# Channel mixing of a hybrid decoder layer: plain products, or seven block products with sums on VectorE

## The chip, the cores and the metric

The kernel runs on one core of a Trainium2 chip. Its time is the device time of one execution in microseconds (us). It is given as the median of several runs, and the trace is of one execution more, recorded by the profiler.

## What is computed

One decoder layer for 1024 tokens of width 1024, all in float32. Two token mixers (an RWKV-7 recurrence and a forgetting attention) are merged, projected and added to the residual stream; then comes the channel mixing, the only part that changes:

```python
h2 = _modulate(x, norm2_g[l], sh2, sc2)                      # (1024 tokens, 1024)
ff_out = jnp.square(jax.nn.relu(h2 @ w_ff1[l])) @ w_ff2[l]   # 1024 -> 4096 -> 1024
x = x + gt2[:, None, :] * ff_out
...
return _rmsnorm(x, final_g)
```

## The kernel before

TensorE multiplies float32 as three products of rounded parts. Each operand is split into a rounded high part and the remainder: ScalarE makes the high part by a copy (`ACT.copy`), VectorE subtracts it from the whole. The helper `mm` (L41) is called three times for each product, high by high, low by high, high by low, and every matmul in the trace has its line. A matmul here is 128x128 weights by 512 columns into one bank of PSUM.

Ahead of the channel mixing stands the output projection (`p_out`, L1095 to L1104), for pairs of 128-token tiles. For each tile VectorE multiplies by the gate (L1108) and adds the residual (L1109), giving x1; SP writes x1 to DRAM (`x1_d`, L1110); then come a sum of squares, a reciprocal root and a scaling of the tile `xr` (L1113). After every fourth tile TensorE transposes (L1120), ScalarE applies scale and shift (L1122) and copies the high part (`hhi`, L1123), VectorE makes the low part (`hlo`, L1124). The channel mixing then holds all of h2, transposed, as `hhi` and `hlo`.

The 4096 hidden channels are 32 blocks of 128. `up(n)` (L1140 to L1152) makes one of them for all 1024 tokens: SP loads 512 KB of `w_ff1` (`wr_f`, L173), it is split (L176, L177), 48 matmuls fill `p_f`, ScalarE takes relu and square (`rl`, `fh`), VectorE makes the low part `fl`. `w2(n)` (L1154 to L1165) loads the 512 KB of `w_ff2` that belong to it (`w2r`), POOL multiplies them by the gate `gt2` (L1157), and they are split (`w2h`, `w2l`). `down(g)` (L1181 to L1198) takes two blocks: for each of 8 token tiles and 2 halves of the output 12 matmuls into one bank `o`, which VectorE adds to `acc` (L1193). `acc` begins as x1, read back from DRAM (L1137). The last two calls are taken together, and `finish(t)` (L1171) normalises a tile and sends it out.

The order is written out by hand at the end of the part: up and down alternate, two blocks each.

```python
for g in range(NG + 1):
    ...
        ups.append(up(2 * g + 2))
    if g < NG - 1:
        down(g, ups[gs], w2s[gs])
    if g < NG:
        ups.append(up(2 * g + 3))
        w2s += [w2(2 * g + 2), w2(2 * g + 3)]
```

A scheduler then fixes the order of each engine's queue, and adds the waits: an engine carries out its queue in order, and a queue of DMA issues (SP's, or POOL's) stands still while its first entry waits.

Of the kernel before, what the change touches and what calls it, by code (L numbers as in the profile page):

```python
# [8 lines left out]
F32 = mybir.dt.float32  # L9
F32R = mybir.dt.float32r  # L10
# [6 lines left out]
P = 128  # L17
# [18 lines left out]
def build(ctx, tc, A, out):  # L36
# [13 lines left out]
    actp = ctx.enter_context(pool(name="actp", bufs=1))  # L50
# [986 lines left out]
    wos = []  # L1037

    def wo_load(dp, k):
        raw = dp.tile([P, D], F32, tag="dr", name=f"wr_out{k}", bufs=4)  # L1040
        POOL.dma_start(raw, wout[k])
        return raw
# [9 lines left out]
    with pool(name="yp", bufs=1) as yp, pool(name="gp", bufs=1) as gp:  # L1052
# [19 lines left out]
        for _ in fill:  # L1072
            pass
        dpa = dax.enter_context(pool(name="dpa", bufs=1, side="right"))
        raws = [wo_load(dpa, k) for k in range(4)]
# [7 lines left out]
    with pool(name="dp", bufs=1) as dp:  # L1083
        for k in range(4, KT):
            wo_split(dp, k, wo_load(dpa, k))
        ssq = dp.tile([P, 8], F32, name="ssq2")
        rs2 = dp.tile([P, 8], F32, name="rs2")
        rtmp = dp.tile([P, 16], F32, name="rtmp2")
        x1s = []
        for t in range(8):  # L1090
            ts_ = slice(t * P, (t + 1) * P)
            if t % 2 == 0:
                os_ = [big(f"p_out{t + i}") for i in range(2)]
                for ks in (range(4), range(4, KT)):
                    for i in range(2):  # L1095
                        tt = slice((t + i) * P, (t + i + 1) * P)
                        for hf in range(2):
                            o, sl = os_[i], slice(hf * 512, hf * 512 + 512)
                            for k in ks:
                                wh, wl = wos[k]  # L1100
                                mm(o[:, sl], hhi[:, k, tt], wh[:, sl], k == 0, False)
                                mm(o[:, sl], hlo[:, k, tt], wh[:, sl], False, False)
                                mm(o[:, sl], hhi[:, k, tt], wl[:, sl], False, k == KT - 1)
            o = os_[t % 2]  # L1104
            xt = dp.tile([P, D], F32, tag="x1", name=f"xr{t}", bufs=5)
            SP.dma_start(xt, x_t[t])
            t1 = dpa.tile([P, D], F32, tag="dr", name=f"t1{t}", bufs=4)
            DVE.tensor_tensor(t1, o, gt1, ALU.mult)  # L1108
            DVE.tensor_tensor(xt, xt, t1, ALU.add)  # L1109
            SP.dma_start(x1_d[t], xt)  # L1110
            ACT.activation(t1, xt, AF.Square, accum_out=ssq[:, t : t + 1])
            rsqrt(rs2[:, t : t + 1], ssq[:, t : t + 1], 1.0 / D, eps1, rtmp[:, 2 * t : 2 * t + 2], 1)
            DVE.tensor_scalar(xt, xt, rs2[:, t : t + 1], None, ALU.mult)  # L1113
            x1s.append(xt)
            if t % 4 == 3:
                sl = slice((t - 3) * P, (t + 1) * P)
                for k in range(KT):
                    hp_ = bank(f"hp{t}_{k}")
                    for i in range(4):
                        PE.transpose(hp_[:, i * P : (i + 1) * P], x1s[t - 3 + i][:, k * P : (k + 1) * P], ident)  # L1120
                    hr = dpa.tile([P, 512], F32, tag="dr", name=f"hr2{t}_{k}", bufs=4)
                    ACT.activation(hr, hp_, AF.Identity, bias=sh2[:, k : k + 1], scale=sc2[:, k : k + 1])  # L1122
                    ACT.copy(hhi[:, k, sl], hr)  # L1123
                    DVE.tensor_tensor(hlo[:, k, sl], hr, hhi[:, k, sl].bitcast(F32), ALU.subtract)  # L1124
    dax.close()


    ff1 = A["w_ff1"].rearrange("o (k p) n -> p (o k) n", p=P)
    ff2 = A["w_ff2"].rearrange("o (k p) n -> (o k) p n", p=P)
    G = 2  # L1130
    with pool(name="fp", bufs=1) as fp:
        fg = gt1
        SP.dma_start(fg, A["final_g"].rearrange("(o n) -> o n", o=1).broadcast_to([P, D]))
        acc = []
        for t in range(8):
            a_ = fp.tile([P, D], F32, name=f"acc{t}")
            SP.dma_start(a_, x1_d[t])  # L1137
            acc.append(a_)

        def up(n):  # L1140
            o = proj(load_w(ff1[:, :, n * P : (n + 1) * P], 0, KT, f"f{n}"), f"p_f{n}")
            rl = fp.tile([P, S], F32, name=f"rl{n}", tag="rl", bufs=2)
            ACT.activation(rl, o, AF.Relu)  # L1143
            if n < NFF - 1:
                fh = fp.tile([P, S], F32R, name=f"fh{n}", tag="fh", bufs=3)
                fl = fp.tile([P, S], F32R, name=f"fl{n}", tag="fl", bufs=3)
            else:
                fh, fl = [wp.tile([P, S], F32R, name=f"f{x}{n}", tag="wraw", bufs=2) for x in "hl"]
            ACT.activation(fh, rl, AF.Square)
            DVE.tensor_tensor(rl, rl, rl, ALU.mult)  # L1150
            DVE.tensor_tensor(fl, rl, fh.bitcast(F32), ALU.subtract)
            return fh, fl  # L1152
# [28 lines left out]
        def down(g, fs, ws):  # L1181
            last, n = g == NG - 1, len(fs)
            for t in range(8):
# [13 lines left out]
                if last:  # L1197
                    finish(t)  # L1198
# [37 lines left out]
```

## Time and profile before

| | us |
|---|---|
| runs | 1756.55, 1750.68, 1753.89 |
| median | 1753.89 |
| the profiled execution, its own time | 1749.61 |
| its span in the trace | 1747.6 |
| output projection ends, channel mixing begins | 1036.25 |
| last matmul ends | 1739.81 |

PE is TensorE's matmuls, DVE VectorE, ACT ScalarE, POOL GpSimd, SP the engine that issues most DMAs. The span is the time from the first to the last instruction; the execution's own time has 2.0 us around it. The page of the profile gives busy time by engine, the span in 40 slices of 43.7 us, and the chain of work that ended last: followed back from the end, at each step to what released it. A group of equal instructions is told by line, engine, operation, output and inputs, with its count, its time and the mean of one.

### The profile page before, as it was taken

The page shows a single profiled execution, that of the slowest core. Times are in us where ns is not written, and L with a number is a line of the kernel's source. Part 1 is how long each engine was busy: PE and PEld are TensorE (multiplying, and loading weights), DVE is VectorE, ACT ScalarE, POOL GpSimd, SP SyncE. Part 2 cuts the span into 40 slices and gives each one's busy share as a digit, 9 for nine tenths or more (in the row PEclk, how much of TensorE's full clock was granted, in tenths as well). Part 3 has the DMA queues.
Part 4 walks back from the last instruction along what each step waited for, and adds up shares of the span by engine and source line. Part 5 has one row for each costly group of instructions (what it writes and reads, how often), then busy time and mean ns, then how long its engine had stood idle before and what let it go on. Part 6 is the DMA issues. An engine that isn't in the chain of part 4 may idle for free.

```text
span 1747.6 us, 21804 instructions
## 1 busy us (share of the span) xinstructions
PE 1671.4 (96%) x8677; PEld 1350.8 (77%) x8677; DVE 971.1 (56%) x1500; ACT 570.3 (33%) x869; POOL 368.3 (21%) x265
## 2 busy tenths in 40 slices
PE   3999999999999999999999999999999999999998
PEld 2767776777777778888877888888888888888886
DVE  6676664647656655766657446444444444444436
ACT  5453342435545523332333323111111111111122
POOL 4310000899990012221100002111111111111100
PEclk9999999999999999999999999999999999999999
DMA  8435335421223278877767134111111111111102
GB/s 249 126 112 154 109 99 161 121 61 61 67 70 103 73 232 240 249 235 232 248 204 247 75 125 137 49 48 49 48 49 49 49 49 49 48 49 48 37 12 96
DMA packets 205907, 197.50 MB, mean 113 GB/s; under 512 B 28113, under 2 KB 170730, under 8 KB 205678
## 3 DMA queue, kind: packets, MB, share of 16 engines
q1 hardware_dynamic: 204302, 189.55, 35.9%
q0 software_dynamic: 1296, 6.29, 1.0%
q8 instruction: 68, 1.11, 0.3%
q14 instruction: 33, 0.27, 0.0%
q10 hardware_dynamic: 208, 0.28, 0.0%
HBM read 148.80 MB, written 43.09 MB: 110 GB/s over the span
## 4 chain that ended last, share of the span: by engine, by line
PE 81%; DVE 5%; DMA 4%; ACT 2%; issue 1%; POOL 0%; SPq 0%; DVEq 0%; ACTq 0%
PE o L41 20%; PE p_f L41 20%; PE p_gb L41 5%; PE p_out L41 4%; PE p_ga L41 3%; PE my L41 3%; PE p_ob L41 2%; PE p_fq L41 2%; PE p_fv L41 2%; PE p_fk L41 2%; PE p_v L41 2%; PE yv L41 2%; PE p_r L41 2%; PE p_k L41 2%; PE tp L818 2%; PE s L41 1%
## 5 line engine op out<-in xcount | busy, mean ns | idle before, releaser
L1193 DVE TENSOR_TENSOR acc<-acc,o 128x512 f32<-128x512 f32 x240 | 162.1, 686 | 193.8 <-PE o L41 193.8
L1157 POOL TENSOR_TENSOR w2r<-w2r,gt 128x1024 f32<-128x1024 f32 x32 | 77.3, 2431 | 721.8 <-DMA w2r<-in_w_ff 721.7
L41 PE MATMUL p_f<-hlo,wh_f 128*128 128x512 f32 x512 | 200.0, 391 | 0.0
L41 PE MATMUL p_f<-hhi,wl_f 128*128 128x512 f32 x512 | 199.6, 390 | 0.0
L41 PE MATMUL p_f<-hhi,wh_f 128*128 128x512 f32 x512 | 199.5, 390 | 0.0
L41 PE MATMUL o<-w2h,fl 128*128 128x512 f32 x496 | 193.4, 390 | 0.0
L41 PE MATMUL o<-w2l,fh 128*128 128x512 f32 x496 | 193.2, 390 | 0.0
L41 PE MATMUL o<-w2h,fh 128*128 128x512 f32 x496 | 193.0, 389 | 0.0
L1143 ACT ACTIVATE rl<-p_f 128x1024 f32<-128x1024 f32 x32 | 32.9, 1028 | 268.4 <-PE p_f L41 268.4
L177 DVE TENSOR_TENSOR wl_f<-wr_f,wh_f 128x1024 fp32r<-128x1024 f32 x32 | 41.1, 1284 | 142.3 <-ACT wh_f L176 142.3
L1163 ACT CAST w2h<-w2r 128x1024 fp32r<-128x1024 f32 x31 | 31.1, 1050 | 251.4 <-PE o L41 251.4
L41 PEld LDWEIGHTS p_f<-hlo,wh_f 128*128 128x128 f32 x512 | 96.1, 188 | 20.4 <-DVE hlo L1124 0.5
L41 PEld LDWEIGHTS p_f<-hhi,wl_f 128*128 128x128 f32 x512 | 96.1, 188 | 20.2
L41 PEld LDWEIGHTS p_f<-hhi,wh_f 128*128 128x128 f32 x512 | 96.1, 188 | 20.0
L41 PEld LDWEIGHTS o<-w2h,fl 128*128 128x128 f32 x496 | 93.1, 188 | 20.0
L41 PEld LDWEIGHTS o<-w2h,fh 128*128 128x128 f32 x496 | 93.1, 188 | 19.8
L41 PEld LDWEIGHTS o<-w2l,fh 128*128 128x128 f32 x496 | 93.1, 188 | 19.5
L638 POOL TENSOR_TENSOR dg<-dg,inv 128x62 f32<-128x62 f32 (+30 forms) x62 | 100.2, 1616 | 4.8
L637 POOL TENSOR_TENSOR inv<-dg 128x62 f32<-128x62 f32 (+30 forms) x62 | 93.0, 1500 | 4.9
L822 DVE TENSOR_TENSOR pl<-tp,ph 128x512 fp32r<-128x512 f32 (+1 forms) x80 | 49.2, 632 | 24.8 <-ACT ph L821 24.6
L700 POOL TENSOR_TENSOR sw<-sbd,wcs 64x256 f32<-64x256 f32 x28 | 22.9, 818 | 168.0 <-DVE sbd L701 137.5
L880 ACT ACTIVATE pt<-pt,sm 128x128 f32<-128x128 f32 (+3 forms) x64 | 49.5, 775 | 24.5 <-DVE sm L878 23.5
(466 smaller groups left out, 3729.8 us busy)
## 6 DMA issues: line engine op xcount, KB each, us to landing
aw<-in_w_ada SPq DMA_DIRECT2D x32, 512.0 KB
wr_f<-in_w_ff SPq DMA_DIRECT2D x32, 512.0 KB
w2r<-in_w_ff SPq DMA_DIRECT2D x32, 512.0 KB
wa<-in_w_ada SPq DMA_DIRECT2D x16, 512.0 KB
sc_d<-scb SPq DMA_DIRECT2D x16, 512.0 KB
sct<-sc_d SPq DMA_DIRECT2D x16, 512.0 KB
x<-in_x SPq DMA_DIRECT2D x8, 512.0 KB
ar_d<-ar SPq DMA_DIRECT2D x4, 1024.0 KB
```

Source lines behind the costliest of these rows:

```text
L41: PE.matmul(o, l, r, start=start, stop=stop)
L177: DVE.tensor_tensor(lo, raw, hi.bitcast(F32), ALU.subtract)
L637: POOL.tensor_tensor(tv, dg[:, 0:s, s : s + 1].broadcast_to([P, s, m]), dg[:, s : s + 1, s + 1 :].broadcast_to([P, s, m]), ALU.mult)
L638: POOL.tensor_tensor(dg[:, 0:s, s + 1 :], dg[:, 0:s, s + 1 :], tv, ALU.add)
L700: POOL.tensor_tensor(sw[rs], cur[rs, :, rs], wcs[rs, :, c : c + 1].broadcast_to([64, 4, 64]), ALU.mult)
L818: PE.transpose(tp[:, x * P : (x + 1) * P], pr[b][:, t * P : (t + 1) * P], ident)
L822: DVE.tensor_tensor(pl[:, 0:w_], tp[:, 0:w_], ph[:, 0:w_].bitcast(F32), ALU.subtract)
L880: ACT.activation(pt[:, 0:n], pt[:, 0:n], AF.Exp, bias=low, scale=-1.0, accum_out=ls[:, b : b + 1])
L1143: ACT.activation(rl, o, AF.Relu)
L1157: POOL.tensor_tensor(raw, raw, gt2, ALU.mult)
L1163: ACT.copy(wh, raw)
L1193: DVE.tensor_tensor(acc[t][:, sl], acc[t][:, sl], o, ALU.add)
```

## The change

The product of two matrices, each cut into 2x2 blocks, is made of seven block products in place of eight, in Winograd's form: sums and differences of the blocks of either factor are multiplied, and the products are summed. This is done for the way up and for the way down.

Up: the factors are the weights of two neighbouring blocks of channels (a "pair", 16 of them: `A11` to `A22` for halves of the input width and the two blocks; S1 to S4 their sums) and the activations (`B11` to `B22` for halves of the width and of the tokens; T1 to T4 their sums). A product is 12 matmuls (`up_product`). The products S1 and S4 go into a bank `y`, S2, S3, A22 and the first one into a bank `x`, the second first one into a bank `z`; between the products ScalarE copies the partial result out of the bank into `ff0` to `ff3`, and VectorE adds the final state to it. In the first two pairs the two are taken through each product together, and T1 to T4 are made in between.

Down: the hidden values are the first factor. Per pair seven operands of 128x512 (`A11`, `A12`, `A22`, S3, S1, S2, S4) are written by POOL's queue to DRAM (`f_put`, 112 of 256 KB). The way down follows the whole way up: 4 groups of 4 pairs, 7 steps each; a step is 4 token tiles of 12 matmuls, with 1 MB of hidden values (`load_a`) and in some steps 1 MB of `w_ff2` (`load_b`) by SP. VectorE multiplies the blocks of `w_ff2` by `gt2` (`scale_b`, which POOL did), makes their sums T, the low parts (`fl`, `wl`), and adds each step's banks to `acc` (`evict`); the residual x1 is added in groups 1 and 2 (`residual`). Step 0 of the way down has its loads and splits within the last pair of the way up (`start_down`, `start_split`).

```diff
+    for t in range(8):
...
+                if t == 4:
+                    for j in range(2):
+                        if ks[0] == 0:
+                            first_ops(j)
+                        else:
+                            for name in ("S1", "S3", "S2", "S4"):
+                                rest_sum(j, name)
...
+    def up_product(o, w, b, start):
+        (wh, wl), (bh, bl) = w, HB[b]
+        for k in range(4):
+            mmx(o, wh[:, k], bh[:, k], start and k == 0, False)
+            mmx(o, wl[:, k], bh[:, k], False, False)
+            mmx(o, wh[:, k], bl[:, k], False, k == 3)
...
+    for k in range(4):
+        DVE.tensor_tensor(t1f[:, k], h2b[0][:, k], hi("B11", k), ALU.subtract)
+        DVE.tensor_tensor(t1f[:, k], t1f[:, k], lo("B11", k), ALU.subtract)
+        DVE.tensor_tensor(t2f[:, k], h2b[1][:, k], t1f[:, k], ALU.subtract)
+        t_split("T1", k, t1f)
...
+    def up_step(j, name):
+        x = X[j]
+        if name == "S1":
+            Y[j] = bank(f"y{j}", "y")
+            up_product(Y[j], rest.pop((j, "S1")), "T1", True)
+            ACT.copy(f_tile(j, 3), Y[j])
+        elif name == "S2":
+            up_product(x, rest.pop((j, "S2")), "T2", False)
+            ACT.copy(f_tile(j, 1), x)
+        elif name == "S4":
+            up_product(Y[j], rest.pop((j, "S4")), "B22", False)
+        elif name == "S3":
+            up_product(x, rest.pop((j, "S3")), "T3", False)
+            DVE.tensor_tensor(Fb[j, 3], x, Fb[j, 3], ALU.add)
+            f_square(j, 3)
+            f_put(j, "A22", Fb[j, 3])
+        else:
+            up_product(x, rest.pop((j, "A22")), "T4", False)
+            ACT.activation(f_tile(j, 2), x, AF.Relu)
+            f_square(j, 2, False)
+            f_put(j, "A12", Fb[j, 2])
...
+    for j in range(2, NPAIR):
+        last = j + 1 == NPAIR
+        if j + 2 < NPAIR:
+            raw_pair(j + 2)
+        if last:
+            start_down()
+        up_step(j, "S1")
...
+        up_step(j, "A22")
...
+    for name in ("S1", "S2", "S4"):
+        f_sum(NPAIR - 1, name)
...
+        STEPS = [
+            ("y", True, "A12", "B21", [(0, 0)]),
+            ("x", True, "A11", "B11", [(0, 0)]),
+            ("y", True, "S1", "T1", [(1, 1)]),
+            ("x", False, "S2", "T2", [(0, 1)]),
+            ("y", False, "S4", "B22", [(0, 1)]),
+            ("x", False, "S3", "T3", [(1, 1)]),
+            ("x", False, "A22", "T4", [(1, 0)]),
+        ]
...
+            if i == 1:
+                scale_b("B11")
+            elif i == 2:
+                scale_b("B12")
+                R["T"] = fp.tile([P, 4, 512], F32, name=f"T_{g}", tag="T", bufs=1)
+                DVE.tensor_tensor(R["T"], R["B12"], R["B11"], ALU.subtract)
...
+            src = R[("B21", "B11", "T", "T", "B22", "B12", "T")[i]]
+            h_, l_ = [to.tile([P, 4, 512], F32R, name=f"w{x}{g}_{i}", tag=f"w{x}", bufs=2) for x, to in (("h", fr), ("l", fp))]
+            split(h_, l_, src)
...
+        for s, (g, i) in enumerate(flat):
+            loads(s + 3)
+            prepare(s + 1)
+            if i == 5 and g + 1 < NG:
+                load_b(g + 1, "B21")
+            if g == NG - 1 and i == 0:
+                fg = dpp.tile([P, D], F32, name="fg", tag="gt1", bufs=1)
+                SP.dma_start(fg, A["final_g"].rearrange("(o n) -> o n", o=1).broadcast_to([P, D]))
+            tag, opens, _, _, to = STEPS[i]
+            fa, wb = ops.pop(s)
+            for t in range(4):
...
+                for half, d in to:
+                    evict(o, t + 4 * half, d, s > 0)
...
+            if g in (1, 2) and i >= 3:
+                residual(4 * (g - 1) + i - 3)
```

What the scheduler makes of it stands in the queues. ScalarE's queue in the middle of the way up, before: casts of the weights down, relu, cast of the weights up, square.

```order
L1163 CAST w2h29_12948<-w2r29_12945 128x1024
L1163 CAST w2h30_13079<-w2r30_13076 128x1024
L1143 ACTIVATE rl29_12931<-p_f29_12882 128x1024
L176 CAST wh_f31_13016<-wr_f31_13014 128x1024
L1149 ACTIVATE fh29_12933<-rl29_12931 128x1024
```

The same queue after, from the end of pair 4 into pair 5 (`ur7` is the raw block of pair 7, `uwhi7` its high part, `y5` the bank of S1 and S4, `x4` and `x5` the banks of the others):

```order
L1320 ACTIVATE ff2_4_9944<-x4_9800 128x512
L1093 CAST A22h_5_9948<-ur5_9665 128x512
L1240 ACTIVATE ff2_4_9944<-ff2_4_9944 128x512
L1239 ACTIVATE ff0_5_9923<-ff0_5_9923 128x512
L1240 ACTIVATE ff0_5_9923<-ff0_5_9923 128x512
L1093 CAST uwhi7_10139<-ur7_9969 128x512
L1307 COPY ff3_5_9985<-y5_9972 128x512
L1093 CAST S1h_6_10018<-S_6_10014 128x512
```

The cast of a raw block of weights (`uwhi7`) now stands ahead of a copy out of PSUM (`ff3_5`), after which TensorE goes on in that bank; before, a bank was read once, when it was complete.

SP's queue where the way up ends. Before, at the end of the part, loads for up and down in turn and the output:

```order
L173 DMA wr_f30_12952<-in_w_ff1 128x8x128
L1156 DMA w2r29_12945<-in_w_ff2 128x1024
L1156 DMA w2r30_13076<-in_w_ff2 128x1024
L173 DMA wr_f31_13014<-in_w_ff1 128x8x128
L1156 DMA w2r31_13083<-in_w_ff2 128x1024
L1179 DMA out_y<-acc0_9071 128x1024
```

After, at the beginning of the way down (`f_d` is the DRAM copy of the hidden operands, `dA1` that of step 1):

```order
L1497 DMA dA3_11639<-f_d_9050 128x4x512
L1555 DMA x1t0_12412<-x1_d_8379 128x1024
L1555 DMA x1t1_12481<-x1_d_8379 128x1024
L1503 DMA B22_0_11641<-in_w_ff2 128x4x512
L1605 DMA fg_13140<-in_final_g 128x1024
L1497 DMA dA1_11633<-f_d_9050 128x4x512
L1503 DMA B11_0_11634<-in_w_ff2 128x4x512
L1497 DMA dA2_11631<-f_d_9050 128x4x512
L1503 DMA B12_0_11632<-in_w_ff2 128x4x512
```

The load of `fg`, written for the last group, has moved ahead of the loads of steps 1 and 2; it takes the memory of the tile `ft15`, whose last write to DRAM it waits for.

VectorE's queue in the way down. Before, evictions one behind the other, with the splits of the next blocks between them:

```order
L1193 TENSOR_TENSOR acc7_9085<-acc7_9085,o8_7_0_11530 128x512
L1193 TENSOR_TENSOR acc7_9085<-acc7_9085,o8_7_1_11538 128x512
L1164 TENSOR_TENSOR w2l19_11619<-w2r19_11615,w2h19_11618 128x1024
L1164 TENSOR_TENSOR w2l20_11878<-w2r20_11874,w2h20_11877 128x1024
L177 TENSOR_TENSOR wl_f21_11815<-wr_f21_11812,wh_f21_11814 128x1024
```

After, around the steps 3 to 5 of group 1:

```order
L1094 TENSOR_TENSOR wl1_4_12357<-B22_1_12134,wh1_4_12356 128x2048
L1583 TENSOR_TENSOR fl11_12353<-dA11_12204,dh11_1_12350 128x1024
L1545 TENSOR_TENSOR acc0_11668<-x1_1_0_12220,acc0_11668 128x512
L1545 TENSOR_TENSOR acc1_11683<-x1_1_1_12234,acc1_11683 128x512
L1556 TENSOR_TENSOR acc0_11668<-acc0_11668,x1t0_12412 128x1024
L1511 TENSOR_TENSOR B21_2_12500<-B21_2_12500,gt2_5349 128x2048
L1545 TENSOR_TENSOR acc2_11698<-x1_1_2_12248,acc2_11698 128x512
L1511 TENSOR_TENSOR B22_2_12630<-B22_2_12630,gt2_5349 128x2048
```

Between the evictions now stand scalings, sums and splits of 128x2048, and the residual.

## Rows read from the trace of the kernel before

**Rows 1.** Page: span, busy time by engine, the span in 40 slices.
```profile
span 1747.6 us, 21804 instructions
...
PE 1671.4 (96%) x8677; PEld 1350.8 (77%) x8677; DVE 971.1 (56%) x1500; ACT 570.3 (33%) x869; POOL 368.3 (21%) x265
...
PE   3999999999999999999999999999999999999998
```

**Rows 2.** The chain of waits from 950 us on: start, us, what.
```profile
1036.25 0.02 issue
...
1043.19 0.76 DVE xr L1113
...
1048.94 24.74 PE p_f L41 x108
1073.68 21.80 PE o L41 x96
...
1739.81 0.02 issue
```

**Rows 3.** Windows: us, busy PE, PEld, DVE, ACT, POOL, granted clock, DMA share, GB/s.
```profile
950.00:955.00 5.00, 3.29 (x12) 1.70 (x10) 4.03 (x6) 3.91 (x5) 0.00 (x0) 0.96 0.86 306
955.00:960.00 5.00, 4.99 (x16) 3.96 (x16) 2.32 (x3) 0.50 (x1) 0.00 (x0) 0.70 0.62 238
...
1044.00:1060.00 16.00, 16.00 (x79) 12.84 (x80) 7.63 (x9) 12.53 (x19) 2.82 (x2) 1.00 0.74 290
...
1200.00:1300.00 100.00, 100.00 (x441) 82.61 (x441) 46.34 (x56) 18.62 (x19) 9.54 (x4) 1.00 0.16 48
```

**Rows 4.** Timeline of DVE, 1205 to 1212 us: start, us, instruction.
```profile
1205.97 0.69 DVE L1193 TENSOR_TENSOR acc<-acc,o 128x512 f32<-128x512 f32 x1 [6.66 <-PE o L41]
1206.57 1.23 DVE L177 TENSOR_TENSOR wl_f<-wr_f,wh_f 128x1024 fp32r<-128x1024 f32 x1
1207.71 1.22 DVE L1150 TENSOR_TENSOR rl<-rl 128x1024 f32<-128x1024 f32 x1
```

**Rows 5.** DVE's groups by shape: count, busy us, mean ns, idle before.
```profile
L1193 DVE TENSOR_TENSOR acc<-acc,o 128x512 f32<-128x512 f32 x240 | 162.1, 686 | 193.8 <-PE o L41 193.8
...
L1164 DVE TENSOR_TENSOR w2l<-w2r,w2h 128x1024 fp32r<-128x1024 f32 x31 | 36.5, 1218 | 0.0
...
L177 DVE TENSOR_TENSOR wl_fv<-wr_fv,wh_fv 128x1024 fp32r<-128x1024 f32 x4 | 9.7, 2418 | 0.3 <-ACT wh_fv L176 0.3
...
L588 DVE TENSOR_TENSOR bk<-bk,wcs 128x2048 f32<-128x2048 f32 x4 | 9.1, 2269 | 0.0
```

**Rows 6.** ACT's groups by shape, the same columns.
```profile
L1163 ACT CAST w2h<-w2r 128x1024 fp32r<-128x1024 f32 x31 | 31.1, 1050 | 251.4 <-PE o L41 251.4
...
L1122 ACT ACTIVATE hr<-hp,sh,sc 128x512 f32<-128x512 f32 x16 | 11.7, 789 | 6.6 <-PE hp L1120 6.6
...
L1123 ACT CAST hhi<-hr 128x512 fp32r<-128x512 f32 x16 | 9.2, 635 | 0.0
```

**Rows 7.** Timelines of SP and of POOL, 1226 to 1234 us: a load, its first use.
```profile
1228.23 1.48 SPq L1156 DMA_DIRECT2D w2r<-in_w_ff  x2
...
1231.52 4.86 POOL L1157 TENSOR_TENSOR w2r<-w2r,gt 128x1024 f32<-128x1024 f32 x2 [38.90 <-DMA w2r<-in_w_ff]
```

**Rows 8.** The same timelines, 1036 to 1075 us.
```profile
1039.75 5.13 SPq L1137 DMA_DIRECT2D acc<-x_d  x8
1052.43 0.81 SPq L1156 DMA_DIRECT2D w2r<-in_w_ff  x2
...
1057.18 5.75 POOL L1157 TENSOR_TENSOR w2r<-w2r,gt 128x1024 f32<-128x1024 f32 x2 [186.12 <-DMA w2r<-in_w_ff]
```

**Rows 9.** Instructions of line 1041, loads by POOL's queue: min, median, max ns; landing.
```profile
L1041 POOL DMA_DIRECT2D wr_out<-in_w_out x8: 540/540/608, 843.8 to 870.5; - x8
...
DMA to landing us min/median/max: 4.4/6.7/9.6
```

More of the change, by code (lines that the diff above doesn't have):

```diff
@@ L1082, in build @@
     x1_d = dram.tile([8, P, D], F32, name="x1_d")
[L1083 to L1124, printed above, removed]
@@ new lines, in build, with f_put, f_tile, f_square @@
+    AOPS = ("A11", "A12", "A22", "S3", "S1", "S2", "S4")
+    f_d = dram.tile([len(AOPS), NPAIR, P, 512], F32, name="f_d")
+    X, Z, Y, Fb, Fs = {}, {}, {}, {}, {}
+    def f_put(j, name, src):
+        POOL.dma_start(f_d[AOPS.index(name), j], src)
+    def f_tile(j, b):
+        Fb[j, b] = up_.tile([P, 512], F32, name=f"ff{b}_{j}", tag=f"ff{b}", bufs=1 if b == 2 else 2)
+        return Fb[j, b]
+    def f_square(j, b, relu=True):
+        f = Fb[j, b]
+        if relu:
+            ACT.activation(f, f, AF.Relu)
+        ACT.activation(f, f, AF.Square)
@@ new lines, in first_second, with first_first, first_out @@
+    def first_second(j):
+        wh, wl = first[j]
+        Z[j] = bank(f"z{j}", "z")
+        up_product(Z[j], (wh[:, 4:8], wl[:, 4:8]), "B21", True)
+    def first_first(j):
+        wh, wl = first[j]
+        X[j] = bank(f"x{j}", "x")
+        up_product(X[j], (wh[:, 0:4], wl[:, 0:4]), "B11", True)
+    def first_out(j, which):
+        if which == 0:
+            ACT.copy(f_tile(j, 0), Z[j])
+        else:
+            DVE.tensor_tensor(Fb[j, 0], X[j], Fb[j, 0], ALU.add)
+            f_square(j, 0)
+            f_put(j, "A11", Fb[j, 0])
@@ L1169, in build @@
         rtmp = fp.tile([P, 16], F32, name="rtmp3")
+        x1ts = {}
+        STEPS = [
[7 more added lines that the diff above has]
+        ]
+        flat = [(g, i) for g in range(NG) for i in range(7)]
@@ new lines, in build, with evict @@
+        seen = set()
+        def evict(o, t, d, scaled):
+            sl = slice(512 * d, 512 * d + 512)
+            if t >= len(acc):
+                acc.extend(fp.tile([P, D], F32, name=f"acc{t_}") for t_ in range(len(acc), t + 1))
+            if (t, d) in seen:
+                DVE.tensor_tensor(acc[t][:, sl], o, acc[t][:, sl], ALU.add)
+            else:
+                seen.add((t, d))
+                if scaled:
+                    ACT.copy(acc[t][:, sl], o)
+                else:
+                    DVE.tensor_tensor(acc[t][:, sl], o, gt2[:, sl], ALU.mult)
@@ L1200, in build @@
[L1200 to L1212 removed]
+        BL = {1: "B11", 2: "B12", 3: "B22"}
```

422 lines of the change are left out of this document (351 added, 71 removed).

## The prediction

> **What bounds the kernel now.** I began with the busy shares and the slices of the span [rows 1]. They say that TensorE (PE) is the engine to save on: it is busy 96% of the span, 9 tenths or more in every slice but the first and the last. Then I followed the chain of waits through the channel mixing, the only part that changes [rows 2]. From 1048.94 us to 1739.81 it is TensorE alone: `p_f`, two blocks up, 96 matmuls, `o`, two blocks down, 96, and so on without a wait between. One matmul of 128x512 takes 21.80/96 = 0.2271 us there. The part starts when the output projection ends, at 1036.25; 3072 matmuls are 697.7 us and 32 transposes some 3.5, of 703.6 us in all, so 2.4 us are lost, all around the last tile `xr7`, which is ready only at 1043.95. The stretches confirm it [rows 3]: between 1200 and 1300, PE 100 of 100 us at the full clock, VectorE (DVE) 46, ScalarE (ACT) 19, GpSimd (POOL) 10, DMA 16%. A saved matmul is thus worth its full 0.2271 us, as long as the other engines, now with room, keep up.
>
> **Matmuls removed.** Seven products replace eight: TensorE's queue has 6868 rows instead of 7252, 384 matmuls of 128x512 fewer. 384 x 0.2271 = **87.2 us** [rows 2]. A pair of channel blocks takes 84 matmuls, 19.1 us; a step down (48) 10.9 us. All else is what the other engines give back of that.
>
> **The opening, +4.5.** The way up needs sums of the activations, T1 to T4, that exist only after the last transpose. TensorE's products with the first half of the tokens, 48 matmuls (10.9 us), cover the wait for `xr7`. From the last transpose to the end of the last T4 split, DVE has 55 operations of 128x512. Back to back such operations start 0.60 us apart [rows 4], though each takes 0.69 [rows 5]: 33.0 to 38 us, plus 0.8 for the first ACT copy out of PSUM [rows 6]. Beside them TensorE has 141 matmuls, 32.0 us, of which about 8 come after the last split. So 33.8 or 38.8 less 30.2: 3.6 to 8.6 us lost, a little more where a copy waits its turn on ACT, against 2.4 lost before. I take 4.5 net; ends +1 and +11.
>
> **The way up, +2.** Per pair DVE has 18 operations of 128x512, 10.8 us at the pitch of [rows 4], and ACT 18 of 0.64 to 0.79 us [rows 6], 12 to 14: both fit in 19.1. What is tight is one load. The raw block of the pair after next may be fetched only when split A22l of this one is done: after the product A22, ACT's relu 0.79, a cast 0.64, DVE's subtraction 0.69 [rows 5, 6], some 2.1 us. On ACT the cast of that block, `uwhi`, stands ahead of the copy `ff3` out of bank y, which TensorE needs before product S4, 36 matmuls or 8.2 us after A22. So the first half, 512 KB, must land within 8.2 - 2.1 - 0.64 - 0.79 = 4.6 us. A load of that size by SP was used 3.3 us after its issue [rows 7], and 4.8 us after it where 4 MB of other loads went ahead [rows 8]. The first costs nothing, the second 0.15 us in each of 13 pairs, 2 us. I take 2; ends 0 and +13 (1 us a pair). The 112 writes of the results into DRAM go through POOL's queue, 0.54 us of issue each [rows 9], 3.8 us a pair on an engine that now does nothing else here.
>
> **From up to down, +15.** This is the new wait. Step 1 down loads operands that only the last pair completes. Count from E0, the end of step 0; the last product up ends 38 matmuls, 8.6 us, earlier. Relu, square and DVE's last difference end at -6.5 (0.79, 0.64, 0.69); its write takes at least 4.4 us, the shortest POOL transfer in the trace [rows 9], and ends at -2.1. On SP's queue the load of `fg` waits for exactly this write, as it takes that tile's memory; behind it stand `dA1`, `B11`, `dA2`, `B12`, 1 MB each, issued by -0.3. One megabyte at the 290 GB/s that the busiest stretch moved [rows 3] is 3.6 us, and 1.5 us is what 3.3 us leaves beside 512 KB at that rate [rows 7]. With half a megabyte of `fg` ahead of them they land at about 4.2, 7.8, 11.4 and 15.0. Then DVE is the chain. An operation of 128x2048 takes 2.27 us [rows 5]; an ACT cast of it some 1.9, from 1.05 for 1024 and 0.64 for 512 [rows 6]. `B11`: scaled 10.1, cast 12.0, subtracted 14.3, where step 1 really begins, its 43 remaining matmuls ending at 24.1. On DVE follow two `fl` (16.6), scaling `B12` (18.9), an eviction and the sum T (21.8), two more evictions and the next sum (25.3), the subtraction for T's low part (27.5): step 2 keeps 40 matmuls for after that and ends at 36.6 instead of 21.8. Stall 15; the bounds are 12 (loads at 390 GB/s, the same bytes at a DMA share of 1 [rows 3]) and 20 (a write of 6.7 us and loads at the pace of [rows 8]). From step 3 on the queues have caught up. **+1.5** for the clock: after TensorE's gap at 951 the granted clock was 0.70 for 5 us [rows 3], and 5 x 0.30 = 1.5 us went with it.
>
> The Trainium skill (page SBUF — State Buffer, section SBUF: two separate sides) warns that GpSimd cannot write a transfer's descriptors while VectorE holds the port that they share, which would delay these writes; by that rule a write could take the 9.6 us that is the trace's longest, and the stall would be the upper bound. The Trainium skill (page DMA: Bandwidth & Descriptors, section Anatomy of one DMA — SWDGE (gpsimd) path) gives 2.0 us + bytes/436 GB/s, an estimate of 2.6 us for 256 KB, and by it the stall is nearer 13; the trace's own POOL transfers of 512 KB (4.4 to 9.6 us) are all above that fit's 3.2.
>
> **The way down, +1, and the end, +1.7.** Per group of seven steps DVE has 28 evictions, 14 `fl`, 15 operations of 128x2048 and in two groups 4 residual sums. At the pitch of [rows 4] (0.60, 1.14, some 2.19): 16.8 + 16.0 + 32.9 + 4.6 = 70 us; by full durations [rows 5] 75; TensorE has 76.3. It fits by a hair; single steps run 2 to 3 us over their 10.9 and lean on what was prepared ahead. I take 1; ends 0 and 8. POOL's multiplication by `gt2`, hidden before, becomes DVE's 16 scalings, counted here. Loads are 11 MB in 76 us, far below what [rows 3] shows possible. At the end DVE's eviction, root and final product of a tile follow on only 12 matmuls (2.7 us) of it, so the last tiles queue a little: I put 1.7 us, an estimate between 0 and 4, on top of the 7.8 that lie now between the last matmul (1739.81) and 1747.6 [rows 1, 2].
>
> **The sum.** -87.2 + 4.5 + 2 + 15 + 1.5 + 1 + 1.7 = -61.5. The profiled execution took 1749.6 us, so 1688.1. That execution is 4.3 below the median of the runs, 1753.9; against the median I say **1692 us**.
>
> **Rivals.**
> 1. The step down is not held up: `fg`'s wait and the DVE chain hide behind step 0. Then 1692 - 15 = 1677. Against it stands the order on SP's queue; for it, that the write is priced by transfers of twice its size. 0.12.
> 2. DVE becomes the bound. What divides 75 us a group from 76 is gone if its operations run 10% over their durations; for it speaks the subtraction `wl_fv`, 2.42 us where `w2l` of the same size takes 1.22, against it that no group of the channel mixing did so [rows 5]. Each group then costs 6 us or so, the opening 4 more: 1692 + 28 = 1720. 0.12.
> 3. Slower than before: the raw block on the way up lands late, and every pair waits, as the cast stands ahead of the copy. Each microsecond over 4.6 costs 13; the gain of 61.5 is used up at a landing of 9.3 us, and the longest landing in the trace is 9.6 (POOL's queue) [rows 9]: 4.6 + 5 gives 1692 + 65 - 2 = 1755. The 16% DMA share of this stretch speaks against it. 0.04.
>
> That the change does less than it says is excluded by the count of rows.
>
> **How the numbers follow.** The forecast has 0.69, the rivals 0.12, 0.12 and 0.04, and 0.03 stays for what I do not see. The bounds of the terms, taken together and not all at their ends, reach from 1674 to 1722, which takes in rivals 1 and 2. A difference of 0.3%, 5 us, is about what a measurement of this kernel can tell from none. The forecast and rivals 1 and 2 are faster by far more, 0.93 together; rival 3 is slower, and of the 0.03 I give 0.02 to no change and 0.01 to slower, which makes 0.05.
>
> **What would show it.** Right: in the chain after 1048, pieces of TensorE with no wait from the second pair to the last; a wait of some 12 us ahead of `x0_1_0`, released by ACT's `wh0_1`, and one of a few us ahead of `y0_2_0` by DVE `wl0_2`; DVE at about 90% in the way down; a granted clock of 0.7 just after the gap. Wrong: TensorE waiting for ACT `ff3` in every pair (rival 3); waits for `fl` or `wl` in each step down (rival 2); no gap at step 1 (rival 1).

## The result, and the profile after

The changed kernel takes **1699.41 us** (median of 1694.67, 1695.92, 1702.90, 1707.88) where the kernel before took 1755.22 beside it: ratio **0.969**, 95% interval 0.9641 to 0.9738. The forecast was 1692, range 1674 to 1722, faster at 0.93. The profiled execution took 1695.92 with a span of 1694.2; the sum had 1688.1 for it.

The page, the lines that answer to [rows 1]:

```profile
span 1694.2 us, 21870 instructions
...
PE 1597.7 (94%) x8293; PEld 1277.9 (75%) x8293; DVE 1129.7 (67%) x1685; ACT 731.2 (43%) x1138; POOL 356.2 (21%) x353
...
PE   3999998999999999999999999999999969999997
...
PEclk9999999999999999999999999999999989999999
```

TensorE (PE) lost 73.7 us of work, VectorE (DVE) and ScalarE (ACT) gained about 160 each. One slice stands out, the 33rd, with PE at 6 tenths and the clock below 9: the change from up to down. The table of PE's waits in the channel mixing (line waited for: total us, times, longest) puts all but 4.0 us of what it lists there; the short waits of the way up, told below, hardly appear in it:

```profile
PE x L1215 <- ACT wh L1093: 14.5, 1, 14.5
PE y L1215 <- ACT T1h L1093: 2.1, 2, 1.3
...
PE y L1215 <- DVE wl L1094: 0.6, 1, 0.6
```

The chain that ended last, through that place (start, us, what):

```profile
1364.32 5.95 DMA f_d<-ft
...
1370.33 0.33 SPq L1605
...
1370.71 6.89 DMA dA<-f_d
...
1378.75 2.36 DVE fl L1583 x2
1381.11 2.21 DVE B L1511
...
1383.35 1.91 ACT wh L1093
...
1385.30 10.75 PE x L1215 x36
...
1398.95 2.21 DVE wl L1094
...
1401.21 9.51 PE y L1215 x40
```

It reads as forecast in its links: the last write to DRAM, `fg` behind it on SP's queue (SPq, L1605), then the loads, then scale and cast for step 1, then the operations for step 2. In one point the order is another: the two `fl` stand ahead of the scaling of `B11` on DVE, and step 1 begins after the cast, not after the subtraction. Windows, the columns of [rows 3], of the way up, the gap, and the fullest group of the way down:

```profile
1200.00:1300.00 100.00, 99.47 (x426) 79.25 (x425) 58.41 (x92) 52.38 (x92) 18.88 (x35) 1.00 0.42 145
...
1376.00:1384.00 8.00, 0.00 (x0) 0.00 (x0) 4.56 (x3) 2.65 (x3) 0.00 (x0) 0.51 1.05 394
...
1487.00:1564.00 77.00, 77.00 (x339) 63.18 (x338) 72.06 (x63) 27.43 (x22) 0.00 (x0) 1.00 0.52 180
```

In the gap the DMA engines are full, at 394 GB/s, and the clock is 0.51, the 1.2 GHz level. In this window of the way down PE is busy all the time, beside a DVE at 94%. In the way up DVE has 42% to spare, and yet a pair lasts 19.7 us where 84 matmuls at 0.2271 are 19.1. The timelines of SP, ACT, DVE and PE over one pair, put together, show a closed loop:

```profile
1206.72 0.37 SPq L1108 DMA_DIRECT2D ur<-in_w_ff  x1
...
1211.22 0.62 ACT L1093 CAST uwhi<-ur 128x512 fp32r<-128x512 f32 x1 [1.61 <-DMA ur<-in_w_ff]
...
1213.93 0.70 DVE L1126 TENSOR_TENSOR S<-ur 128x512 f32<-128x512 f32 x1 [1.37 <-DMA ur<-in_w_ff]
...
1218.28 0.68 DVE L1325 TENSOR_TENSOR ff<-y,ff 128x512 f32<-128x512 f32 x1
...
1220.33 0.69 DVE L1339 TENSOR_TENSOR fs<-ff,ff 128x512 f32<-128x512 f32 x1 [0.77 <-ACT ff L1240]
1220.94 0.68 DVE L1315 TENSOR_TENSOR ff<-x,ff 128x512 f32<-128x512 f32 x1
...
1221.68 0.50 PE L1215 MATMUL x<-T4h,A22h 128*128 128x512 f32 x1 [0.21 <-DVE ff L1315]
...
1225.87 0.69 DVE L1094 TENSOR_TENSOR A22l<-ur,A22h 128x512 fp32r<-128x512 f32 x1 [1.46 <-ACT A22h L1093]
...
1226.59 0.92 SPq L1108 DMA_DIRECT2D ur<-in_w_ff  x2
```

The first half of the raw block was used 4.5 us after its issue (forecast limit 4.6), the second half 7.2 us after it. Behind that second half stand seven DVE operations, then the addition of bank y (L1325), ACT's two passes over it, the sum S3 (L1339) that waits for them, and the addition that reads bank x (L1315), which must be over before product A22 may go on in x. After A22 come the relu, a cast and A22l, and only then the next load: 1226.59 - 1206.72 = 19.87 us around. Pair 14 is the control: no raw block is left to fetch, cast and sum beside it, and it takes 19.41 us, which is what its matmuls alone take (below).

Where the profiled execution's time went, beside the sum (from the end of `p_out` at 1035.64; the channel mixing's matmuls at 0.2271 us taken off each stretch):

| term | forecast | measured |
|---|---|---|
| opening, to product S1 of pair 2 | +4.5 | 4.9 lost against 2.4 before: +2.5 |
| way up | +2 | 2.2 (pair 2) + 12 x 0.63 + 0.8 (last pair): +10.6 |
| from up to down, with the clock | +16.5 | +18.2 |
| way down, 25 steps | +1 | +2.2 |
| end, 8.8 us after the last matmul | +1.7 | +1.0 |

The differences are +8.8; what lies ahead of the part and around the span was 0.9 shorter, which leaves the 7.8 by which the execution missed the sum.

Since the unchanged part ahead of the channel mixing ends up to 12 us apart in the profiled executions (the last `p_out` starts between 1032.4 and 1044.9 us), those below are compared by **the stretch**: from the start of the last `p_out` matmul to the end of the span. It is 711.8 us before (1035.84 to 1747.6) and 659.0 after (1035.25 to 1694.2). A stretch is one execution, and it scatters too: pair 2 took between 21.0 and 22.7 us in these kernels, in no pattern that follows the edits. A difference of under 2 us in the stretch says nothing by itself. By their medians alone most single edits can't be told from the changed kernel.

### The profile page after: what moved, and what is told of

Same layout as the page of the kernel before. It is cut to its first block, busy times and chain, and to the rows that moved or that the text cites. A ratio compares the mean times of both kernels' runs of the same rounds, so it can differ in the third digit from the quotient of the medians.

```text
span 1694.2 us, 21870 instructions
## 1 busy us (share of the span) xinstructions
PE 1597.7 (94%) x8293; PEld 1277.9 (75%) x8293; DVE 1129.7 (67%) x1685; ACT 731.2 (43%) x1138; POOL 356.2 (21%) x353
## 4 chain that ended last, share of the span: by engine, by line
PE 62%; issue 14%; DVE 7%; DMA 6%; POOL 3%; ACT 2%; SPq 0%; POOLq 0%; DVEq 0%; ACTq 0%
PE x L1215 11%; PE y L1215 8%; PE p_gb L41 5%; PE p_out L41 5%; PE p_ga L41 3%; POOL f_d L1230 3%; PE my L41 3%; PE p_fk L41 3%; PE p_ob L41 3%; PE p_fq L41 2%; PE p_fv L41 2%; PE yv L41 2%; PE p_v L41 2%; PE p_r L41 2%; PE tp L819 2%
## 5 line engine op out<-in xcount | busy, mean ns | idle before, releaser
L1404 ACT CAST dh<-dA 128x1024 fp32r<-128x1024 f32 x54 | 56.3, 1046 | 148.0 <-PE x L1215 72.2
L1215 PE MATMUL x<-wh,dh 128*128 128x512 f32 x256 | 102.1, 399 | 14.5 <-ACT wh L1093 14.5
L1215 PE MATMUL x<-wl,dh 128*128 128x512 f32 x256 | 100.9, 395 | 0.0
L1215 PE MATMUL x<-wh,fl 128*128 128x512 f32 x256 | 100.1, 391 | 0.0
L1583 DVE TENSOR_TENSOR fl<-dA,dh 128x1024 fp32r<-128x1024 f32 x54 | 65.2, 1218 | 20.7 <-ACT dh L1404 14.7
L1215 PE MATMUL y<-wh,dh 128*128 128x512 f32 x176 | 69.4, 394 | 0.0
L1215 PE MATMUL y<-wl,dh 128*128 128x512 f32 x176 | 68.6, 393 | 0.6 <-DVE wl L1094 0.6
L1215 PE MATMUL y<-wh,fl 128*128 128x512 f32 x176 | 68.3, 388 | 0.0
L1215 PEld LDWEIGHTS x<-wh,fl 128*128 128x128 f32 x256 | 48.7, 190 | 10.7
L41 PE MATMUL p_out<-h_wo,hhi 128*128 128x512 f32 x128 | 50.8, 397 | 2.2 <-ACT h_wo L1050 2.2
L41 PE MATMUL p_gb<-hhi,wl_gb 128*128 128x512 f32 x128 | 51.4, 402 | 0.2 <-DVE wl_gb L178 0.2
```

Of the source, the lines that this page charges most:

```text
L41: PE.matmul(o, l, r, start=start, stop=stop)
L1215: PE.matmul(o, l, r, start=start, stop=stop, skip_group_check=True)
L1404: ACT.copy(hs[i], src[:, 2 * i : 2 * i + 2])
L1583: DVE.tensor_tensor(fl[:, sl], src[:, sl], f32(hs[i_]), ALU.subtract)
```

## The experiments

### fg by POOL's queue

```diff
-                SP.dma_start(fg, A["final_g"].rearrange("(o n) -> o n", o=1).broadcast_to([P, D]))
+                POOL.dma_start(fg, A["final_g"].rearrange("(o n) -> o n", o=1).broadcast_to([P, D]))
```

> Only the queue that loads fg changes, from SP to POOL; all work stays. Theory (SP's queue stands still behind fg, which waits for the last write of the way up): dA1 is issued some 6 us earlier, right after B22, and B11 as soon as its own memory is free, 2.3 us before the end of step 0. TensorE's wait ahead of step 1 (14.5 us, released by wh0_1) shrinks to 7 to 8 us, the half clock behind it is shorter, and the whole is 7 to 9 us faster than the changed kernel. Rival (the loads share the bandwidth with B22 and land no sooner; or the chain scale, cast, subtract alone sets the wait): the wait stays above 12 us and the time moves by under 3 us.

Measured: 1700.21 us, ratio 0.9704 [0.9679, 0.9729]; the stretch is 660.3, though pairs 2 and 3, which this edit does not touch, account for 2.4 us more than in the changed kernel. The rival held. The wait ahead of step 1:

```profile
PE x L1215 <- ACT wh L1093: 13.3, 1, 13.3
```

and the chain at that place:

```profile
1375.88 11.48 DMA dA<-f_d
```

`dA1` was now issued 5.9 us ahead of the end of step 0, but landed after 11.5 us in place of 6.9, with the DMA engines at a share of 1.04 and 391 GB/s (window 1382 to 1394). `x1t1` and `B22` had been issued within 1 us ahead of it, `B11`, `dA2`, `B12` and `fg` some 4 to 5 us behind it. At that rate the 2.5 MB up to and with `dA1` would take 6.7 us in turn. So these loads shared the rate, where the prediction let them land one after another. If so, the bytes in flight, and not the place in SP's queue, bound the gap; the next experiment tests that. `fg`'s wait, which the prediction put at the head of the chain, is worth 1.2 us of 14.5.

### B11 fetched early

```diff
-            to, tag = {"B11": (fr, "B11"), "B12": (fr, "B12"), "B21": (dpr, "ur"), "B22": (fp, "B22")}[name]
+            to, tag = {"B11": (fp, "B11"), "B12": (fr, "B12"), "B21": (dpr, "ur"), "B22": (fr, "B22")}[name]
...
-            if g or name not in ("B11", "B12"):
+            if g or name not in ("B22", "B12"):
...
-            SP.dma_start(x1t, x1_d[t])
+            POOL.dma_start(x1t, x1_d[t])
```

with `fg` as in the first experiment.

> As the run before, and besides the residual tiles are loaded by POOL's queue, and the blocks B11 and B22 change places, so that B11 of the first group lies in memory that is free before the way up ends and B22 in that which step 0 holds. All work stays. Theory (the wait ahead of step 1 is load, then DVE and ACT on B11; nothing else is late): B11 is scaled and split beside step 0, what is left ahead of step 1 is dA1's own cast and subtraction, 2 to 4 us after step 0 (its tiles are held by step 0), nothing ahead of step 2; 12 to 16 us faster than the changed kernel. Rival (DVE is the bound in the way down and has to make these operations up later): waits of the same sum reappear in steps 2 to 6, under 8 us gained.

Measured: 1694.69 us, ratio 0.9671 [0.9634, 0.9709]; the stretch is 652.4, 6.6 less than the changed kernel's. The wait fell from 14.5 to

```profile
PE x L1215 <- ACT dh L1404: 5.9, 1, 5.9
```

so fewer bytes in the gap do shorten it; the gain is about half of the 12 to 16 us expected. It is under the 8 us of the rival, but the waits that the rival put into steps 2 to 6 did not come: behind step 1 PE waits 0.8 us once. The rest is queue order: `B11` was there, but its scaling stands on DVE behind the evictions of step 0, whose last product ended at 1372.98:

```profile
1373.01 0.69 DVE acc L1551
1373.70 2.21 DVE B L1511
```

### The sum S3 on POOL

```diff
-        DVE.tensor_tensor(dst, a, b, op)
+        (POOL if name == "S3" and j > 1 else DVE).tensor_tensor(dst, a, b, op)
```

> On the way up the sum S3 of the results (one of four, from pair 2 on) is made by POOL instead of VectorE. Theory (in every pair product A22 waits because VectorE's addition out of bank x stands in its queue behind the sum S3, which waits for a square on ScalarE): the wait of 0.2 to 0.4 us ahead of A22 goes in 14 pairs, a pair takes 19.4 us instead of 19.75, 4 to 5 us in all. Rival (POOL and VectorE get in each other's way when both read SBUF, or the matmuls' own pitch is what makes a pair 19.75): VectorE's operations of 128x512 grow over 0.69 or the pair stays within 0.1 us of 19.75.

Measured: 1698.86 us, ratio 0.9687 [0.9655, 0.972]; the stretch is 656.3, 2.7 less, where 4 to 5 were expected. Pairs 3 to 14 run at 19.39 to 19.41 us in place of 19.41 to 19.87, 3.6 us in all, of which pair 2 took 1.3 back in this execution; the wait ahead of A22 is gone. One operation of 0.69 us, taken out of DVE's order, opens the loop; DVE's share of the time was never the point. From here the pair is 84 matmuls and nothing else, but at 0.231 us each, not 0.2271.

### Why the matmuls are longer: patterns

In the changed kernel the interval of matmuls depends on the product: 0.2278 (x with `uw`), 0.2290 (z), 0.2303 (S1), 0.2301 (A22), 0.2333 (S2, S4 and S3), and 0.2290 in a step down.

The first try was a kernel of matmuls alone, whose output is not the layer's: 24, 12 and 6 into a bank, banks opened or added to, both orders of the three, DVE or ACT busy beside them or reading PSUM, and zeros as data.

> No part of the layer: only matmuls of 128x512 in the patterns of both kernels, 96 each, on loaded data and then on zeros, and three patterns beside a busy VectorE, a busy ScalarE and a VectorE that reads PSUM; the output is not the layer's. It measures the interval of matmuls, 0.2271 us before, 0.2283 to 0.2333 on the way up of the changed kernel, 0.2290 on its way down, though neither clock nor waits differ. If the pattern sets it (how many matmuls go to a bank, whether a bank is opened or added to, the order of high and low parts): one pattern differs from another by 1 to 3% with nothing beside it. If work beside it sets it: all patterns alone within 0.5%, and more beside a busy engine. If the data set it: loaded data slower than zeros.

Measured: all alike, 84 or 96 matmuls in 19.04 or 21.76 us, 0.2267 each. None of the three held.

### Both edits together

> The two edits that helped, together: fg and x1t by POOL's queue with B11 fetched early, and the sum S3 on POOL. They act at different places (the one at the transition, 6.5 us of the stretch after the output projection; the other once a pair, 0.33 us each, 2.7 us of that stretch), so by the theory they add: about 9 us less than the changed kernel from the last p_out to the end, some 650 us. The rival, that the gain of the one is only slack for the other (both end on DVE's queue at the last pair), gives 652.4, that of the transition alone.

Measured: 1688.74 us, ratio 0.9629 [0.9607, 0.9652]; the stretch is 647.9, 11.1 less than the changed kernel's, where 6.6 and 2.7 were had singly. They add; the rival's 652.4 did not come.

### Step 0 not begun within the way up

```diff
             nx[x] = dpr.tile([P, 4, 512], F32, name=f"d{x}0", tag=tag, bufs=1)
+            ACT.copy(nx[x][:, 0, 0:1], Fb[NPAIR - 1, 2][:, 0:1])
             SP.dma_start(nx[x], src)
...
-        if last:
-            start_down()
...
-        else:
-            nx["A"] = start_split(0)
...
-        else:
-            nx["B"] = start_split(1)
...
         up_step(j, "A22")
...
+    start_down()
+    nx["A"] = start_split(0)
+    nx["B"] = start_split(1)
```

The added copy of one column goes into the tile that the load then fills, so that the load waits for the last result.

> Step 0 of the way down has its loads issued and its operands split only after the last product of the way up has begun to be read out, by a tiny ScalarE copy that needs the last result; nothing else changes. If the early start is what keeps TensorE busy at the change of direction, 38 matmuls of step 0 no longer cover the 8.6 us after the last product: two loads of 1 MB (about 7 us), casts and subtractions come before step 0, some 23 us from the last product up to the end of step 0 in place of 8.6; the wait of step 1 shrinks from 14.5 to about 6, since its write and loads go on meanwhile: 4 to 12 us longer in all, 6.5 likeliest. If the early start is worth nothing (the chain of loads and DVE work behind the last write sets the start of step 1 anyway), the time is the changed kernel's within 1 us.

Measured: 1711.34 us, ratio 0.9743 [0.9724, 0.9763]; the stretch is 668.6, 9.6 more, within the 4 to 12 expected. Two waits take the place of one, and a second stretch at half clock comes with the second (a window, columns as above):

```profile
PE y L1215 <- ACT dh L1405: 12.6, 1, 12.6
PE x L1215 <- ACT wh L1093: 7.2, 1, 7.2
...
1396.00:1406.00 10.00, 4.92 (x11) 3.61 (x12) 8.04 (x6) 3.79 (x3) 0.00 (x0) 0.50 0.83 308
```

So the early start of step 0 is worth about 10 us: its 38 last matmuls cover 8.6 us of the gap, and its loads stay out of it. The waits grew by 5.3 us; some 3 us more went with the clock, as TensorE was busy 6.3 and 4.9 us in two stretches at half clock, in place of 4.7 us in one; the last us is not accounted for.

### Scalings by gt2 on POOL

```diff
-            DVE.tensor_tensor(raws[name], raws[name], by_gt2(int(name[2]) - 1), ALU.mult)
+            eng = POOL if gs > 0 else DVE
+            eng.tensor_tensor(raws[name], raws[name], by_gt2(int(name[2]) - 1), ALU.mult)
```

> The scalings by gt2 in groups 1 to 3 go from DVE to POOL, where the kernel before had them: about 2.2 us less on DVE for each of 12, 26 us in all, in the stretch where DVE is busy 84 to 94%. Theory: DVE at 94% is not the bound, as the trace shows no wait of TensorE in the way down, so the time stays within 1.5 us of the changed kernel's, and the matmul's interval of 0.229 us stays too. Rival (DVE is the bound in a hidden way, by matmuls slowed or small gaps): 26 us less on DVE would give several us, 4 to 10.

Measured: 1710.19 us, ratio 0.9739 [0.9718, 0.9759]; the stretch is 669.7, 10.7 **more**. Both expectations were wrong. DVE lost 27.4 us of scalings, and its other operations took longer. The groups of two lines in the way down, first of the changed kernel, then of this one (count: duration in ns, min/median/max):

```profile
L1583 DVE TENSOR_TENSOR fl<-dA,dh x50: 1204/1218/1228, 1401.7 to 1668.9; 128x1024 fp32r<-128x1024 f32 x50
...
L1094 DVE TENSOR_TENSOR wl<-B,wh x14: 2281/2285/2293, 1415.2 to 1654.2; 128x2048 fp32r<-128x2048 f32 x14
```

```profile
L1584 DVE TENSOR_TENSOR fl<-dA,dh x50: 1205/1214/5637, 1408.3 to 1685.9; 128x1024 fp32r<-128x1024 f32 x50
...
L1094 DVE TENSOR_TENSOR wl<-B,wh x14: 2272/2282/6685, 1425.3 to 1671.2; 128x2048 fp32r<-128x2048 f32 x14
```

and from the timelines of POOL and DVE of this one:

```profile
1504.78 10.96 POOL L1512 TENSOR_TENSOR B<-B,gt 128x2048 f32<-128x2048 f32 x2 [23.52 <-DMA B<-in_w_ff]
...
1511.79 5.04 DVE L1584 TENSOR_TENSOR fl<-dA,dh 128x1024 fp32r<-128x1024 f32 x1
```

The medians are unchanged; single operations take 4 to 5 us more, while POOL multiplies. The evictions, with one operand in PSUM, stay at 0.68. Steps down that start late cost 8.1 us together, most of it at one place, around step 3. There DVE's operations, held up by the first scaling, make PE wait 1.4 and 1.6 us, and the granted clock then stood at half:

```profile
1420.00:1427.00 7.00, 6.00 (x14) 4.73 (x15) 7.00 (x5) 3.87 (x5) 0.00 (x0) 0.51 0.21 64
```

Of these 6.0 us of TensorE work some 3 are the clock's. In the last thirteen steps the matmuls' interval was 0.2333 in place of 0.2290 (13 x 48 x 0.0043 = 2.7 us); why is open. The Trainium skill (page SBUF — State Buffer, section SBUF: two separate sides) says that GpSimd and a DVE operation with two SBUF inputs share a port pair as an exclusive lock, where the loser stands for the whole instruction; the rows agree: the `fl` that started at 1511.79 ended 1.1 us after POOL did, about its own 1.22 us. It fits the one slow row that spoke for rival 2 as well, `wl_fv` at a mean of 2.42 us in [rows 5]: three of the four stood beside operations of POOL's in the recurrence and took 4.42, 2.41 and 1.63 us, the fourth had POOL idle and took 1.22. In the channel mixing before, a `rl` beside a multiplication by `gt2` took 3.42 us, at a median of 1.22.

### Why the matmuls are longer: places

> Products of 12 matmuls alone, with operands at the same places of SBUF as in the changed kernel (the eight products of the way up and one of the way down), then the products in the order of a pair, without and with copies out of the banks by ScalarE and VectorE, and with more work beside them. The output is not the layer's. If the place of the operands sets the interval between matmuls, products alone show 0.228 to 0.233 us, each as in the changed kernel. If the order of a pair (changes of bank within an accumulation, copies from the banks) sets it, only the later parts show it. If it is neither, all show 0.2267, and the cause is something else that runs beside.

Measured, the chain of waits, products of 72 matmuls alone, here S1, S2, A22 and the step down:

```profile
29.28 16.36 PE wy L63 x72
45.64 16.80 PE wx L63 x72
...
112.39 16.36 PE wxa L63 x72
128.75 16.50 PE wdn L63 x72
```

and, in the order of a pair without copies, one S2 (bank `x`), and S1 (bank `y`) and S2 of the next pair:

```profile
285.84 2.80 PE bx L63 x12
...
302.48 2.76 PE by L63 x12
305.25 2.80 PE bx L63 x12
```

S2 takes 16.80/72 = 0.2333 us with nothing beside it, S4 and S3 the same, and the step down 0.2292: there the place is enough. S1, A22 and the first products take 0.2272 alone, less than in the changed kernel. In the order of a pair they take the kernel's times, S1 2.76/12 = 0.230, and the pair 305.25 - 285.84 = 19.41 us, with no copy and no other engine at work; copies and more work beside it change nothing. So the intervals come from places and order together. The places that this kernel copies are, modulo 256 bytes: the weights of S1 to S4 and A22 at 160, T1 and T4 too, but T2 and what S4 and S3 multiply at 96; in a step down `wh` at 160, `dh` at 96, `wl` and `fl` at 0.

The next kernel separated relative from absolute place:

> Accumulations of 48 matmuls, weights all at one place of SBUF and moving operand all at one place; the place of the weights shifted by 0, 32, 64, 96, 128 and 256 bytes against four shifts (0, 32, 64, 96) of the moving operand; then weights or moving operand at the high end of SBUF, and weights alternating between two places. The output is not the layer's. In the run before this one the products alone took 0.2271 us a matmul where weights and moving operand have the same address modulo 128 bytes and 0.2333 where they differ by 64. Theory: the relative alignment sets the interval; equal shifts modulo 128 give 0.227, a difference of 64 gives 0.233, whatever the distance. Rival (absolute place): the slow products were those with weights high in SBUF; then the shifts change nothing and the runs at the high end take 0.233.

Measured, 48 matmuls each; `a64b0` is weights shifted by 64 bytes, moving operand by 0; in `hm` the moving operand lies at the high end of SBUF:

```profile
32.64 10.89 PE a0b0e L63 x48
...
54.72 11.20 PE a64b0e L63 x48
...
77.16 11.16 PE a128b0e L63 x48
88.32 10.88 PE a256b0e L63 x48
...
166.15 11.00 PE a0b64e L63 x48
...
299.31 11.16 PE hw L63 x48
310.48 10.89 PE hm L63 x48
...
365.45 11.11 PE bth L63 x48
```

Equal places modulo 256 bytes: 0.2267 to 0.2275. Weights 64 bytes below: 0.2292. Every other shift tried: 0.2325 to 0.234. The theory held, with a period of 256 and not 128 bytes. The absolute place does nothing: weights at the high end (`hw`) took 11.16 us, as the rival said, but lie 128 bytes off modulo 256, and `a128b0` took the same. One run limits the rule: in `bth` weights and moving operand of each matmul have equal places, but every second matmul lies 64 bytes further, and the interval is 0.2315. So the neighbours in the queue count as well; how is open.

### The places put right

```diff
     dpp = ctx.enter_context(pool(name="dpp", bufs=1, side="right"))
+    dpp.tile([P, 16], F32, name="pad1")
...
+        fp.tile([P, 24], F32, name="pad2")
         ssq = fp.tile([P, 16], F32, name="ssq3")
```

Two unused tiles, 160 bytes: in the changed kernel, and in the one with both earlier edits.

> The changed kernel with two unused tiles, of 64 bytes on the right side of SBUF and 96 bytes ahead of the way down's pool, so that weights and moving operand of all its products lie at equal addresses modulo 256 bytes; the order of every queue is the same. If alignment is what made matmuls longer than 0.2271 us: intervals of all products of the way up and of the steps down at 0.227, 0.33 us a pair (5 us, of which the wait ahead of product A22 may take back up to its 0.36 a pair) and 0.09 a step down (2.5 us), so 3 to 8 us less from the last p_out to the end, the 7.8 likeliest where nothing else binds. If the bank's changes or the other engines' traffic made them longer, the intervals stay at 0.228 to 0.233 and the time is the changed kernel's within 1 us.

> The kernel of both earlier edits (fg, x1t and B11 early, sum S3 on POOL) with the same two unused tiles. It has no wait ahead of A22, so by the theory of alignment all of 7.8 us come off the stretch from the last p_out to the end; by the other theory nothing does.

Measured: the changed kernel with the tiles takes 1698.55 us, ratio 0.9682 [0.9657, 0.9707]: no difference that these runs can tell. Its matmuls do run at 0.2267 and a step down at 10.88 us, but the pair stays at 19.76 us, since it goes around the loop, and the wait ahead of A22 has grown by what the matmuls save:

```profile
PE x L1216 <- DVE ff L1316: 4.8, 11, 0.7
```

The stretch is 657.1, 1.9 less, below the 3 to 8 expected: I had let the wait take back 0.36 a pair at most. What is gained lies behind the way up: from product S1 of the last pair to the last matmul it takes 2.3 us less, and only there do the matmuls set the time. Pair 14, without a load, took 19.04 us here too. With the loop open, in the other kernel, everything is paid out: ten of the pairs 3 to 14 at 19.04 us, which is 84 x 0.2267, steps down at 10.88, the stretch 641.1, 6.8 less than with both edits (7.8 expected). That kernel takes **1681.07 us**, ratio **0.9581** [0.9559, 0.9603], the fastest of all here.

## Why the prediction was right, and where it was off

- **Matmuls removed, 87.2.** By count it held: 384 fewer. By price the step of 0.2271 us for every matmul was off: in the changed kernel they took 0.2278 to 0.2333. The places of the new tiles shifted weights against moving operands, which no row of before could show.
- **The opening, +4.5: measured +2.5**, inside its ends of +1 and +11. The waits of PE there are 0.2 to 1.3 us each.
- **The way up, +2: measured +10.6.** This is the term that was mis-sized, though inside its ends of 0 and +13. Its place was right, the raw block that may be fetched only after A22l. The prediction followed the first half to the copy `ff3` and found 4.6 us of room; that half took 4.5 and cost nothing. The second half, which lands 2.7 us later, starts the operations of DVE behind which the addition out of bank x stands. So rival 3's mechanism, every pair late by the load, did act, at another place: 0.3 us of the 0.63 lost in a pair are the loop's, the rest the longer matmuls'. The sign "no wait from the second pair to the last" did not come true. The loop (19.7) and the longer matmuls (19.4) lie over one another, and the loop hides what shorter matmuls gain: the sum S3 on POOL gave 0.3 us a pair, the places alone none, both together 0.66.
- **From up to down, 15 + 1.5: measured 18.2.** The wait is 14.5 us ahead of `x0_1_0` after ACT's `wh0_1`, and 0.6 ahead of `y0_2_0` after DVE's `wl0_2`, as listed under what would show it, though the second was put at a few us. The parts differ from the sum's and partly cancel, so that its closeness is in part luck: the last write took 6.0 us and not 4.4; the loads shared 394 GB/s in place of landing in turn at 290, and so `dA1` took 6.9 us (the sum's own terms put its landing at 4.8, where 4.2 is written); but step 1 did not have to wait for the subtraction. `fg`, put at the head, is worth 1.2 us. The clock stood at 0.5 in the gap, and at half clock until about 1390 the first matmuls of step 1 lost some 2.3 us (half of the 4.7 from 1385.3 on) in place of 1.5. Rival 1 fell.
- **The way down, +1: measured +2.2**, and not by DVE: even at 94% it made no matmul wait. 25 steps at 10.99 in place of 10.90 us are 2.2 us, the places again. Rival 2 fell. That DVE took the scalings from POOL, counted by the prediction only as work, is the better side of it: on POOL they cost 10.7 us, 2.7 of them by the interval that is left open.
- **The end, +1.7: measured +1.0.**
- **The rule weighed there** (the Trainium skill, page SBUF — State Buffer, section SBUF: two separate sides), by which VectorE can hold up a write's descriptors: the last write took 6.0 us, 5.4 in the runs with S3 on POOL and with `fg` on POOL's queue, and 8.6 with `B11` early, near the 9.6 us taken as the worst. The five writes just ahead of it took 2.3 to 2.7 us in the changed kernel, close to the estimate of 2.6 weighed in the prediction. The loads `x1t1` and `B22` were issued within 0.3 us of the last write; in the run with `B11` early, with the DMA engines at a share of 1.00, all six last writes took 5.9 to 8.7. Loads beside the writes fit these rows without the rule; no run here separates the two.

## What to carry to other kernels

Where an engine with room to spare holds up the one that bounds, look for a closed loop: from a load, through every operation that stands ahead in the queues, back to the point that frees the load's buffer. Its length, not any busy share, is the period, and it hides gains made elsewhere until it is opened. Loads in flight together share the rate, so the first to be needed should be issued while little else flows. And after any change of tile sizes, check the matmul's interval product by product: two unused tiles of 160 bytes were worth 6.8 us here once the loop was open, and nothing on the way up while it was closed.

## What the runs showed of the hardware

- The interval of 128x512 float32 matmuls is 0.2267 us where weights and moving operand of a whole accumulation have equal SBUF addresses modulo 256 bytes, 0.2292 where the weights are 64 bytes below, 0.2325 to 0.234 at the other shifts tried. The Trainium skill (page SBUF — State Buffer, section SBUF: two separate sides) says that TensorE never waits on anyone at SBUF; these rows show up to 3% that hangs on where its own two operands lie; that its two reads meet would fit, and is not shown. What a mixture of shifts gives is not settled: matmuls with equal places each, alternating by 64 bytes, took 0.2315, and the products down took 0.2290 and, in the run with scalings on POOL, whose edit moves no tile, 0.2333.
- Loads that are in flight together share the rate: 1 MB of `dA1` took 6.9 us beside `fg` and three loads of its size (394 GB/s), and 11.5 us where `x1t1` and `B22` were in flight as well (391 GB/s).
- A multiplication of 128x2048 on POOL (4.6 to 6.6 us) made DVE subtractions of 1.2 us take up to 5.6, and those of 2.3 up to 6.7.
